# Transposing head rows in 32x32 blocks on VectorE, with the transfers to DRAM placing the blocks

## The chip, the cores and the metric

One core of a Trainium2 chip runs the whole kernel. The metric is device time in microseconds for one launch; lower is better. Engines are TensorE (PE; its weight loads are listed as PEld), VectorE (DVE), ScalarE (ACT), GpSimd (POOL) and SyncE (SP), which here issues nearly all transfers. Sixteen DMA engines move the data; their share in the profile is the mean over all of them.

## The reference

The reference computes one step of a decoder layer for 256 prompt tokens and 8 sequences of 8 sample tokens (320 tokens, D = 2048, float32). Two token mixers work on the same projection and are merged:

```python
proj = einsum('btd,de->bte', x, w_in)     # split into the heads' inputs and gates
h, C, n, m = _mlstm(q, k, v, ig, lf, C0, n0, m0)         # 4 heads, DK 256, DV 512
h = _unheads((h - mu) * rsqrt(var + eps)) * ml_norm_g
branch_a = h * sigmoid(ml_o)
o, S = _hgrn2(hq, log(f), 1 - f, i, S0)                  # 8 heads, DK 128, DV 256
o = _unheads(o * rsqrt(mean(o * o) + eps)) * hg_norm_g
branch_b = o * silu(hg_g)
merged = sigmoid(gate_a) * (branch_a @ w_branch_a) + sigmoid(gate_b) * (branch_b @ w_branch_b)
x1 = layernorm(alpha * x + merged @ w_out)
y = layernorm(alpha * x1 + relu(x1 @ w_up)**2 @ w_down)
```

The outputs are y and the last states of every head: for the prompt C (a sum over tokens of weighted key times value), n, m and S, and the same for the samples.

## The kernel before, in words

The weights stream through as 304 tiles of 2048 x 128 (`TILES`). A tile gives 128 output features for all 320 tokens: 16 steps along the contraction, and in each step three float32r products (high by high, low by high, high by low), 48 products of 320 columns. Half a tile, 512 KB, is one unit: SyncE loads it into one of three raw buffers (`wr`, `reload`), ScalarE writes its high part (`prep`, `wh`), VectorE its low part (`low_half`, `wl`), TensorE uses it (`run_main`, products recorded at line 340, `mm`). Later other buffers (`bb`) take the place of `wh` and `wl`.

The order of tiles: for each of the 4 mLSTM heads its values, keys and queries (`mv`, `mk`, `mq`) and two gate tiles; four more gate tiles; for each of the 8 HGRN heads two gate tiles and its inputs (`hf`, `hq`, `hi`); then the output gates (`o`), rest of the merge gates, `hg` with `wa`, `wb`, `wo`, and the feed-forward tiles `up` and `dn`.

Everything else is side work in chains (Python generators), which a planner (`Sched`) puts between the weight products on each engine, with estimated costs and due times. The order on each engine is thereby written out before launch; at run time an engine waits only on semaphores. SyncE's queue is in order too: a transfer whose data isn't ready holds up those behind it.

The tokens stand along the free axis of the projections, features along the partitions. A head's result has tokens along the partitions, and the branches need features there. So `turned`, called at the end of `m_sample` for the mLSTM rows and of `h_out` for the HGRN rows, turns blocks of 128 x 128 on TensorE (line 1280) into a PSUM bank. ScalarE evicts them, with the norm's weight of each feature (`vec`, columns `V_MLG` and `V_HGG`) as the scale, and SyncE stores them to DRAM (`hT`, `oT`). Samples of two heads share one block: an even head's sample rows wait in the third part of `hb` or `on` until the odd head's are added, and the odd head turns both. `fetch` reads the stored blocks back much later, when the output gates' tiles come (`ev_o`, `ev_hg`), where VectorE multiplies them with the gate.

The prompt's keys are turned too, for the last states: `m_KW` turns the weighted mLSTM keys (line 1072), splits them into high and low part, and `m_CP` stores them with the values (`kD`, `vD`); `h_sp` turns the HGRN keys (line 1671) and stores them in `sD`. The products of keys and values are made at the very end (`m_C`, which loads by GpSimd's queue, and `h_S`).

Line 334 is the helper `A` (every ScalarE activation), line 343 the helper `dma` (every SyncE transfer), line 502 the low part of a weight unit.

Of the kernel before, what the change touches and what calls it, by code (L numbers as in the profile page):

```python
# [20 lines left out]
TOK = 320  # L21
# [221 lines left out]
def rel(pool, item):  # L243
    return ("rel", pool, item)
# [51 lines left out]
class Program:  # L296
# [49 lines left out]
    def carve(self):  # L346
# [38 lines left out]
        self.vs = Pool([R(512)])  # L385
        self.khl = Pool([R(1024).rearrange("p (x s k) -> p x s k", x=2, s=2)])
        self.kst = Pool([R.three(2, 256)])
# [10 lines left out]
        self.on = Pool([self.on0])  # L398
        self.ho = Pool([B(320) for _ in range(2)])
        R2 = Part(self.ra, 5120)  # L400
# [13 lines left out]
    def carve_h(self):  # L414
        C = self.Part(self.pool.tile([128, F3], F32, name="f3h", tag="f3"))
        qz = C(ODD + 256)
        self.hqz = Pool([qz])
        pp = C(512)
        self.pp = Pool([pp])
        self.ktk = Pool([C.three(2, 128)])  # L420
# [236 lines left out]
    def start(self):  # L657
# [52 lines left out]
        self.gb_ev = [Ev() for _ in range(KT)]  # L710
        self.hT = [self.dr.tile([128, TOK], F32, name=f"hT{j}") for j in range(KT)]
        self.oT = [self.dr.tile([128, TOK], F32, name=f"oT{j}") for j in range(KT)]
        self.hT_ev = [Ev() for _ in range(KT)]
# [56 lines left out]
    def lb(self):  # L770
# [284 lines left out]
    def m_KW(self, h):  # L1055
# [12 lines left out]
        khl = yield acq(self.khl)  # L1068
        b = yield acq(self.sbank)
        for i in range(2):  # L1070
            for c in range(2):
                yield ("pe", PE_T, lambda: nc.tensor.transpose(b[:, 256 * i + 128 * c:256 * i + 128 * c + 128], kw[:, c, 128 * i:128 * i + 128], self.ident))  # L1072
# [104 lines left out]
    def m_C(self, h):  # L1177
        k = yield acq(self.kx)
        kt = yield ("pool", 1000, lambda: self.nc.gpsimd.dma_start(k, self.kD[h]))
        w = yield acq(self.vx)  # L1180
# [28 lines left out]
    def m_sample(self, h):  # L1209
# [54 lines left out]
        yield rel(self.sm, dn)  # L1264
        yield from self.turned(4, odd, hb, 4 * h, V_MLG, self.tst, self.hT, self.hT_ev)
        yield rel(self.hb, hb)
# [7 lines left out]

    def turned(self, n, odd, rows, j0, vec, pool, to, ev):

        for j in range(n):
            b = yield acq(self.sbank)
            for i in range(2 + odd):
                yield ("pe", PE_T, lambda: self.nc.tensor.transpose(b[:, 128 * i:128 * i + 128], rows[:, i, 128 * j:128 * j + 128], self.ident))  # L1280
            jj = j0 + j
            o = yield acq(pool)
            g = lambda i: self.vec[:, vec + i:vec + i + 1]
            yield ("act", act(NP_, True, 1), lambda: self.A(o[:, 0:NP_], b[:, 0:NP_], scale=g(jj)))
            if odd:
                yield ("act", act(64, True, 1), lambda: self.A(by_row(o, NP_, False), by_row(b, NP_ + ODD, True), scale=g(jj)))
                e = yield acq(pool)
                yield ("act", act(64, True, 1), lambda: self.A(by_row(e, 0, False), by_row(b, NP_, True), scale=g(jj - n)))
            yield rel(self.sbank, b)
            k = TOK if odd else NP_  # L1290
            yield ("sp", 620, lambda: self.dma(to[jj][:, 0:k], o[:, 0:k]))
            if odd:
                yield ("sp", 620, lambda: self.dma(to[jj - n][:, NP_:TOK], e[:, 0:64]))
                yield post(ev[jj])
                yield post(ev[jj - n])
            yield wait(self.later(2500))
            yield rel(pool, o)
            if odd:
                yield rel(pool, e)

# [359 lines left out]
    def h_sp(self, h):  # L1660
# [7 lines left out]
        yield ("dve", dve(256), lambda: v.tensor_tensor(ks, qk[:, 0, 0:256], ks, ALU.mult))  # L1668
        b = yield acq(self.sbank)
        for i in range(2):  # L1670
            yield ("pe", PE_T, lambda: nc.tensor.transpose(b[:, 128 * i:128 * i + 128], ks[:, 128 * i:128 * i + 128], self.ident))  # L1671
        kt = yield acq(self.ktk)
        yield ("act", act(256, True), lambda: self.A(kt, b[:, 0:256].rearrange("p (a k) -> p a k", a=2)))
        yield rel(self.sbank, b)
# [44 lines left out]
    def h_out(self, h):  # L1719
# [31 lines left out]
        yield rel(self.at, at)  # L1751
        yield from self.turned(2, h % 2, on, 2 * h, V_HGG, self.ho, self.oT, self.oT_ev)
        yield rel(self.on, on)
# [23 lines left out]
    def fetch(self, kind, j):  # L1777

        src, ev = dict(o=(self.hT, self.hT_ev), wa=(self.gaD, self.m_ev), hg=(self.oT, self.oT_ev), wb=(self.gbD, self.gb_ev))[kind]
        e = self.got[kind, j] = Ev()  # L1780
        yield wait(ev[j])
        x = self.met[kind, j] = yield acq(self.ld)
        e.t = (yield ("sp", 620, lambda: self.dma(x, src[j]))) + 3000.0

# [4 lines left out]
    def ev_o(self, j, c, b):  # L1789
# [35 lines left out]
    def ev_hg(self, j, c, b):  # L1825
# [273 lines left out]
    def run(self, pool):  # L2099
# [9 lines left out]
        self.s_ev, self.s_bank = [Ev() for _ in range(HH)], {}  # L2109
        self.sD = [self.dr.tile([128, 768], F32, name=f"sD{j}") for j in range(HH)]  # L2110
        self.kD = [self.dr.tile([128, 2, 2, 256], F32, name=f"kD{j}") for j in range(MH)]
        rows = lambda name, n, k: [self.dr.tile([32 * NB, k], F32, name=f"{name}{j}") for j in range(n)]
# [57 lines left out]
def take_out(r):  # L2170
# [4 lines left out]
        c(y[:NP_].reshape(1, NP_, D)), c(y[NP_:].reshape(NB, NT, D)),  # L2175
        c(r["Cp"].transpose(0, 2, 1, 3).reshape(1, 1, MH, DK, DV)),
        c(n[:, 0:8].reshape(128, MH, 2).transpose(1, 2, 0).reshape(1, 1, MH, DK)),
# [24 lines left out]
```

## Time and profile before

| what | value |
|---|---|
| median of 3 runs | 2295.9 us (2295.43 to 2297.25) |
| profiled execution, its own time | 2295.59 us |
| its span in the trace | 2293.8 us |
| TensorE busy | 2285.9 us, 15706 products |
| VectorE, ScalarE busy | 1403.3 us, 1028.2 us |
| granted TensorE clock | 0.999 |
| DMA packets, data moved | 158303, 434.98 MB |

A row of a group of instructions names line, engine, operation, output and inputs, shape and count, then the busy time of the group and the mean of one in ns, then the idle time of the engine before them and what ended it. In a tile's view a row shows the count, and minimum, median and maximum of the durations in ns. Matmuls are pipelined: durations of neighbours overlap, and the distance between starts is what one adds to the stream.

### The profile page before, as it was taken

What the parts mean: (1) busy time and instruction counts of PE and PEld (TensorE: products, weight loads), DVE (VectorE), ACT (ScalarE), POOL (GpSimd) and SP (SyncE); (2) the same over time, 40 slices, a digit from 0 to 9 for tenths busy, and PEclk for the clock granted to TensorE, in tenths of its full rate; (3) what the DMA queues carried; (4) which work ended last, traced back from release to release, by engine and by line L of the source; (5) the groups of instructions that cost most, each with busy time, mean ns of one, the idle gap of its engine ahead of it and who ended that gap; (6) DMA issues with size and microseconds to landing.
All of it is one profiled execution on the core that took longest, in us unless ns stands there. A gap on an engine that the chain in (4) does not pass through costs nothing.

```text
span 2293.8 us, 39115 instructions
## 1 busy us (share of the span) xinstructions
PE 2285.9 (100%) x15706; PEld 2248.9 (98%) x15706; DVE 1403.3 (61%) x2437; ACT 1028.2 (45%) x1606; POOL 11.3 (0%) x42
## 2 busy tenths in 40 slices
PE   9999999999999999999999999999999999999998
PEld 9999999999999999999999999999999999999998
DVE  7666657788878876555555769544444444444555
ACT  5344445555555555444433547433443343234434
POOL 0000000000000000000000000000000000000000
PEclk9999999999999999999999999999999999999999
DMA  7887876666666565555555654444444444444555
GB/s 239 314 273 263 290 253 206 200 214 204 202 208 223 186 195 175 174 176 172 170 174 185 215 159 143 153 152 151 147 151 153 147 149 154 148 148 153 192 188 184
DMA packets 158303, 434.98 MB, mean 190 GB/s; under 512 B 19868, under 2 KB 50724, under 8 KB 157096
## 3 DMA queue, kind: packets, MB, share of 16 engines
q1 hardware_dynamic: 156968, 426.18, 56.2%
q0 software_dynamic: 1152, 6.29, 0.8%
q8 instruction: 123, 2.02, 0.4%
q14 instruction: 60, 0.49, 0.1%
HBM read 376.25 MB, written 56.15 MB: 189 GB/s over the span
## 4 chain that ended last, share of the span: by engine, by line
PE 98%; DMA 1%; ACT 1%; DVE 0%; issue 0%; SPq 0%; ACTq 0%
PE bank L340 97%; DMA wr<-wt 1%; PE bank L1280 0%; ACT f3m L334 0%; DVE bb L502 0%; PE bank L1551 0%; PE bank L982 0%; ACT oC L334 0%; ACT bb L334 0%; PE bank L1018 0%; PE bank L1671 0%; PE bank L1099 0%; PE bank L1072 0%; ACT wh L334 0%; DVE wl L502 0%
## 5 line engine op out<-in xcount | busy, mean ns | idle before, releaser
L340 PE MATMUL bank<-xh,wh 128*128 128x320 f32 x2408 | 770.7, 321 | 0.2 <-ACT wh L334 0.2
L340 PE MATMUL bank<-xh,wl 128*128 128x320 f32 x2408 | 743.5, 310 | 0.0
L340 PE MATMUL bank<-xl,wh 128*128 128x320 f32 x2408 | 740.4, 309 | 0.0
L334 ACT ACTIVATE wh<-wr 128x1024 fp32r<-128x1024 f32 (+1 forms) x431 | 452.3, 1049 | 594.2 <-PE bank L340 579.9
L502 DVE TENSOR_TENSOR wl<-wr,wh 128x1024 fp32r<-128x1024 f32 x423 | 517.7, 1224 | 328.2 <-ACT wh L334 323.0
L340 PEld LDWEIGHTS bank<-xh,wh 128*128 128x128 f32 x2408 | 452.5, 188 | 7.7 <-issue 3.9
L340 PEld LDWEIGHTS bank<-xl,wh 128*128 128x128 f32 x2408 | 453.1, 188 | 2.6
L340 PEld LDWEIGHTS bank<-xh,wl 128*128 128x128 f32 x2408 | 452.9, 188 | 0.0
L334 ACT ACTIVATE bb<-wr 128x1024 fp32r<-128x1024 f32 x179 | 189.8, 1061 | 358.2 <-PE bank L340 343.0
L502 DVE TENSOR_TENSOR bb<-wr,bb 128x1024 fp32r<-128x1024 f32 x179 | 219.1, 1225 | 165.4 <-ACT bb L334 165.4
L340 PE MATMUL bank<-xh,bb 128*128 128x320 f32 (+1 forms) x1280 | 284.1, 309 | 0.0
L340 PE MATMUL bank<-ra,bb 128*128 128x320 f32 x1264 | 283.3, 308 | 0.0
L340 PE MATMUL bank<-rxb,bb 128*128 128x320 f32 x1112 | 255.0, 309 | 0.0
L340 PE MATMUL bank<-ra,wh 128*128 128x320 f32 x892 | 248.8, 308 | 0.0
L340 PEld LDWEIGHTS bank<-xh,bb 128*128 128x128 f32 x1280 | 214.7, 188 | 0.0
L340 PEld LDWEIGHTS bank<-ra,bb 128*128 128x128 f32 x1264 | 210.6, 188 | 0.2
L340 PE MATMUL bank<-xl,bb 128*128 128x320 f32 (+1 forms) x640 | 197.5, 309 | 0.0
L340 PEld LDWEIGHTS bank<-rxb,bb 128*128 128x128 f32 x1112 | 188.4, 188 | 0.2
L340 PE MATMUL bank<-rxb,wl 128*128 128x320 f32 x596 | 183.7, 308 | 0.0
L340 PE MATMUL bank<-rxb,wh 128*128 128x320 f32 x596 | 183.7, 308 | 0.0
L340 PEld LDWEIGHTS bank<-ra,wh 128*128 128x128 f32 x892 | 161.4, 188 | 0.0
L340 PEld LDWEIGHTS bank<-xl,bb 128*128 128x128 f32 x640 | 120.2, 188 | 0.0
(328 smaller groups left out, 2187.0 us busy)
## 6 DMA issues: line engine op xcount, KB each, us to landing
wr<-wt SPq DMA_DIRECT2D x602, 512.0 KB
rx<-C SPq DMA_DIRECT2D x34, 256.0 KB
Cs<-rx SPq DMA_DIRECT2D x34, 256.0 KB
f<-C SPq DMA_DIRECT2D x30, 256.0 KB
Cs<-f SPq DMA_DIRECT2D x30, 256.0 KB
f<-xT SPq DMA_DIRECT2D x26, 160.0 KB
vD<-ra SPq DMA_DIRECT2D x4, 1024.0 KB
f<-S SPq DMA_DIRECT2D x8, 512.0 KB
```

Source lines behind the costliest of these rows:

```text
L334: return self.nc.scalar.activation(out, in_, func, **kw)
L340: self.nc.tensor.matmul(*a, **kw)
L502: self.V().tensor_tensor(lo, raw, hi.bitcast(F32), ALU.subtract)
```

## The change

Prompt rows in `turned`, the mLSTM keys in `m_KW` and the HGRN keys in `h_sp` are no longer turned by TensorE. VectorE transposes within 32 x 32 blocks, SBUF to SBUF, and the store puts each block in its place in DRAM: one store for each group of 32 partitions, with runs of 32 elements (128 B), or 64 (256 B) for the mLSTM keys. Only the sample rows of a pair of heads still go through TensorE and ScalarE (in the odd head). The norms' weights are no longer a scale of the eviction; they are a factor in `ev_o` (there negated, in place of the constant -1) and `ev_hg`. `hT` and `oT` become one tensor for each head, `kD` holds the keys by token, `skD` is new and takes the HGRN keys out of `sD`. The mLSTM keys' channels stand in another order in `kD`, and the host puts the rows of C back in order.

```diff
@@ carve
-        self.tst = Pool([B(320) for _ in range(2)])
+        self.tst = Pool([B(512)])
+        self.tail = Pool([B(64) for _ in range(2)])
...
@@ lb
+        g = self.vec[:, V_MLG:V_MLG + 16]
+        yield ("dve", 80, lambda: nc.vector.tensor_scalar(g, g, -1.0, None, ALU.mult))
...
@@ m_KW
-        b = yield acq(self.sbank)
-        for i in range(2):
-            for c in range(2):
-                yield ("pe", PE_T, lambda: nc.tensor.transpose(b[:, 256 * i + 128 * c:256 * i + 128 * c + 128], kw[:, c, 128 * i:128 * i + 128], self.ident))
-        bv = b.rearrange("p (a k) -> p a k", a=2)
-        yield ("act", act(512, True), lambda: self.A(kh, bv))
-        yield ("dve", dve(512, True), lambda: v.tensor_tensor(kl, bv, kh.bitcast(F32), ALU.subtract))
-        yield rel(self.sbank, b)
+        by = lambda x, c: x.rearrange("p (b c e) -> p c b e", c=2, e=32)[:, c]
+        st = yield acq(self.stg)
+        for c in range(2):
+            x = kw[:, 0, 0:256] if c else st
+            yield ("dve", dve(256), lambda: v.transpose(x, kw[:, c, 0:256]))
+            x = x.rearrange("p (b e) -> p b e", e=32)
+            yield ("act", act(256), lambda: self.A(by(kh, c), x))
+            yield ("dve", dve(256), lambda: v.tensor_tensor(by(kl, c), x, by(kh, c).bitcast(F32), ALU.subtract))
+        yield rel(self.stg, st)
...
@@ m_CP
-        yield ("sp", 620, lambda: self.dma(self.kD[h], m["khl"].bitcast(F32)))
+        for x in range(2):
+            for a in range(4):
+                yield ("sp", 620, lambda: self.dma(
+                    self.kD[h][x].rearrange("(b r) k -> r b k", r=32)[:, :, 64 * a:64 * a + 64],
+                    m["khl"][32 * a:32 * a + 32, x, :].bitcast(F32).rearrange("r (b k) -> r b k", k=64)))
...
@@ m_C
-        kt = yield ("pool", 1000, lambda: self.nc.gpsimd.dma_start(k, self.kD[h]))
+        kt = yield ("pool", 1000, lambda: self.nc.gpsimd.dma_start(k, self.kD[h].rearrange("x (s p) k -> p x s k", s=2)))
...
@@ turned, new body
+        v = self.nc.vector
+        o = yield acq(pool)
+        for i in range(2):
+            x = o if i == 0 else rows[:, 0, :]
+            yield ("dve", dve(128 * n), lambda: v.transpose(x, rows[:, i, :]))
+            for a in range(4):
+                at = 128 * i + 32 * a
+                yield ("sp", 620, lambda: self.dma(
+                    to[-1].rearrange("(b r) t -> r b t", r=32)[:, :, at:at + 32], x[32 * a:32 * a + 32].rearrange("r (b t) -> r b t", t=32)))
+        t = self.later(2500)
+        for j in range(n if odd else 0):
             b = yield acq(self.sbank)
+            yield ("pe", PE_T, lambda: self.nc.tensor.transpose(b[:, 0:128], rows[:, 2, 128 * j:128 * j + 128], self.ident))
+            for k in range(2):
+                e = yield acq(tail)
+                yield ("act", act(64, True), lambda: self.A(by_row(e, 0, False), by_row(b, ODD * (1 - k), True)))
+                if k:
+                    yield rel(self.sbank, b)
+                yield ("sp", 620, lambda: self.dma(to[-1 - k][128 * j:128 * j + 128, NP_:TOK], e))
+                self.s.spawn(self.back(tail, e), 0)
...
@@ h_sp
-        for i in range(2):
-            yield ("pe", PE_T, lambda: nc.tensor.transpose(b[:, 128 * i:128 * i + 128], ks[:, 128 * i:128 * i + 128], self.ident))
-        yield ("act", act(256, True), lambda: self.A(kt, b[:, 0:256].rearrange("p (a k) -> p a k", a=2)))
-        yield ("sp", 620, lambda: self.dma(self.sD[h][:, 0:256], kt))
-        yield ("sp", 620, lambda: self.dma(self.sD[h][:, 256:768], m["iv"][:, 0:512]))
+        yield ("dve", dve(256), lambda: v.transpose(kt, ks))
+        for a in range(4):
+            p = slice(32 * a, 32 * a + 32)
+            yield ("sp", 620, lambda: self.dma(self.skD[h].rearrange("(b r) k -> r b k", r=32)[:, :, p], kt[p].rearrange("r (b k) -> r b k", k=32)))
+        yield ("sp", 620, lambda: self.dma(self.sD[h], m["iv"][:, 0:512]))
...
@@ h_S
-        t = yield ("sp", 620, lambda: self.dma(x, self.sD[h]))
+        yield ("sp", 620, lambda: self.dma(x[:, 0:256].rearrange("p (i k) -> p i k", i=2), self.skD[h].rearrange("(i p) k -> p i k", i=2)))
+        t = yield ("sp", 620, lambda: self.dma(x[:, 256:768], self.sD[h]))
...
@@ ev_o
-        yield ("dve", dve(TOK), lambda: v.scalar_tensor_tensor(g, g, -1.0, x, ALU.mult, ALU.mult))
+        yield ("dve", dve(TOK), lambda: v.scalar_tensor_tensor(g, g, self.vec[:, V_MLG + j:V_MLG + j + 1], x, ALU.mult, ALU.mult))
...
@@ ev_hg
-        yield ("dve", dve(TOK), lambda: v.tensor_tensor(g, g, x, ALU.mult))
+        yield ("dve", dve(TOK, ptr=1), lambda: v.scalar_tensor_tensor(g, g, self.vec[:, V_HGG + j:V_HGG + j + 1], x, ALU.mult, ALU.mult))
```

More of the change, by code (lines that the diff above doesn't have):

```diff
@@ L398, in carve @@
         self.on = Pool([self.on0])
-        self.ho = Pool([B(320) for _ in range(2)])
+        self.ho = Pool([B(256) for _ in range(2)])
+        self.tail2 = Pool([B(64) for _ in range(2)])
         R2 = Part(self.ra, 5120)
@@ L419, in carve_h @@
         self.pp = Pool([pp])
-        self.ktk = Pool([C.three(2, 128)])
+        self.ktk = Pool([C(256)])
         R = self.Part(self.pool.tile([128, 2320], F32R, name="f2r", tag="f2a"))
@@ L710, in start @@
         self.gb_ev = [Ev() for _ in range(KT)]
-        self.hT = [self.dr.tile([128, TOK], F32, name=f"hT{j}") for j in range(KT)]
-        self.oT = [self.dr.tile([128, TOK], F32, name=f"oT{j}") for j in range(KT)]
+        self.hT = [self.dr.tile([512, TOK], F32, name=f"hT{j}") for j in range(MH)]
+        self.oT = [self.dr.tile([256, TOK], F32, name=f"oT{j}") for j in range(HH)]
         self.hT_ev = [Ev() for _ in range(KT)]
@@ L1264, in m_sample @@
         yield rel(self.sm, dn)
-        yield from self.turned(4, odd, hb, 4 * h, V_MLG, self.tst, self.hT, self.hT_ev)
+        yield from self.turned(4, odd, hb, self.tst, self.tail, self.hT[h - odd:h + 1], self.hT_ev[4 * h - 4:4 * h + 4])
         yield rel(self.hb, hb)
@@ L1273, in m_sample @@
             yield ("sp", 620, lambda: self.dma(self.d["n_out"][:, 8:72], self.nso_flat))
-    def turned(self, n, odd, rows, j0, vec, pool, to, ev):
-        for j in range(n):
-            b = yield acq(self.sbank)
[L1279 to L1299, printed above, removed]
@@ new lines, in turned @@
+    def turned(self, n, odd, rows, pool, tail, to, ev):
+        v = self.nc.vector
[9 more added lines that the diff above has]
+        for j in range(n if odd else 0):
+            b = yield acq(self.sbank)
+            yield ("pe", PE_T, lambda: self.nc.tensor.transpose(b[:, 0:128], rows[:, 2, 128 * j:128 * j + 128], self.ident))
[6 more added lines that the diff above has]
+                self.s.spawn(self.back(tail, e), 0)
+        if odd:
+            for x in ev:
+                yield post(x)
+        yield wait(t)
+        yield rel(pool, o)
@@ L1301, in m_done, with back @@
+    def back(self, pool, x):
+        yield wait(self.later(2500))
+        yield rel(pool, x)
     def m_done(self, h, name, evs, pool):
@@ L1751, in h_out @@
         yield rel(self.at, at)
-        yield from self.turned(2, h % 2, on, 2 * h, V_HGG, self.ho, self.oT, self.oT_ev)
+        yield from self.turned(2, h % 2, on, self.ho, self.tail2, self.oT[h - h % 2:h + 1], self.oT_ev[2 * h - 2:2 * h + 2])
         yield rel(self.on, on)
@@ L1782, in fetch @@
         x = self.met[kind, j] = yield acq(self.ld)
[L1783 removed]
+        n = len(src)
+        y = src[j * n // KT]
+        o = 128 * (j % (KT // n))
+        e.t = (yield ("sp", 620, lambda: self.dma(x, y[o:o + 128, :]))) + 3000.0
     def fetched(self, kind, j):
@@ L2109, in run @@
         self.s_ev, self.s_bank = [Ev() for _ in range(HH)], {}
-        self.sD = [self.dr.tile([128, 768], F32, name=f"sD{j}") for j in range(HH)]
-        self.kD = [self.dr.tile([128, 2, 2, 256], F32, name=f"kD{j}") for j in range(MH)]
+        self.sD = [self.dr.tile([128, 512], F32, name=f"sD{j}") for j in range(HH)]
+        self.skD = [self.dr.tile([256, 128], F32, name=f"skD{j}") for j in range(HH)]
+        self.kD = [self.dr.tile([2, 256, 256], F32, name=f"kD{j}") for j in range(MH)]
         rows = lambda name, n, k: [self.dr.tile([32 * NB, k], F32, name=f"{name}{j}") for j in range(n)]
@@ L2175, in take_out @@
         c(y[:NP_].reshape(1, NP_, D)), c(y[NP_:].reshape(NB, NT, D)),
-        c(r["Cp"].transpose(0, 2, 1, 3).reshape(1, 1, MH, DK, DV)),
+        c(r["Cp"].reshape(MH, 2, 2, 32, 2, DV).transpose(0, 2, 4, 1, 3, 5).reshape(1, 1, MH, DK, DV)),
         c(n[:, 0:8].reshape(128, MH, 2).transpose(1, 2, 0).reshape(1, 1, MH, DK)),
```

4 lines of the change are left out of this document (1 added, 3 removed).

## The prediction

> **What bounds the kernel now.** I read the page first, then the busy time by stretches, then the single products in the timeline, and last the transfers.
>
> ```profile
> span 2293.8 us, 39115 instructions
> PE 2285.9 (100%) x15706; PEld 2248.9 (98%) x15706; DVE 1403.3 (61%) x2437; ACT 1028.2 (45%) x1606; POOL 11.3 (0%) x42
> PE 98%; DMA 1%; ACT 1%; DVE 0%; issue 0%; SPq 0%; ACTq 0%
> ```
>
> TensorE carries 98% of the chain that ended last. A busy share of 100% could still hide waiting, because products overlap, so the pace has to be looked at.
>
> ```profile
> 57.00:115.00 58.00, 58.00 (x398) 52.83 (x398) 36.86 (x73) 23.30 (x39) 0.00 (x0) 1.00 0.89 315
> 115.00:229.00 114.00, 114.00 (x789) 108.49 (x787) 73.18 (x148) 51.90 (x92) 0.00 (x0) 1.00 0.80 268
> 459.00:573.00 114.00, 114.00 (x812) 111.69 (x811) 93.24 (x247) 60.82 (x127) 0.88 (x3) 1.00 0.64 209
> 1400.00:1700.00 300.00, 300.00 (x2048) 300.00 (x2047) 156.01 (x206) 124.09 (x170) 0.00 (x0) 1.00 0.47 151
> ```
>
> The columns are the stretch, its length, then busy time and count of PE, PEld, DVE, ACT and POOL, the granted clock, the DMA share and GB/s. From 1400 to 1700 us there are only weight products: 300 us by 2048 is 0.1465 us for one. The stretches from 57 to 573 us are where the changed work lies (mLSTM heads, then HGRN heads). There TensorE has no idle stretch either, VectorE is busy up to 82% (93.24 of 114) and the 16 DMA rings up to 0.89. So every instruction taken off TensorE there is time, as long as the weights still come in time. The weights are what the rest must not disturb.
>
> **The transposes that go.** These are the groups of transposes in question:
>
> ```profile
> L1280 PE MATMUL bank<-cst,f 128*128 128x128 f32 x80 | 21.7, 271 | 0.0
> L1671 PE MATMUL bank<-cst,f 128*128 128x128 f32 x12 | 3.3, 272 | 0.0
> L1072 PE MATMUL bank<-cst,f2a 128*128 128x128 f32 x16 | 4.3, 272 | 0.0
> L1671 PE MATMUL bank<-cst,f3h 128*128 128x128 f32 x4 | 1.1, 272 | 0.0
> ```
>
> That is 80 in `turned`, 16 for the mLSTM keys, 12 and 4 for the HGRN keys: 112. The changed `turned` keeps a transpose for the sample rows of a pair of heads: 4 blocks by 2 odd mLSTM heads and 2 blocks by 4 odd HGRN heads, 16. So 96 go. A duration of 271 ns isn't the price of one, since the next product starts long before its end; the starts tell it:
>
> ```profile
> 126.04 0.31 PE L340 MATMUL bank<-xh,wl 128*128 128x320 f32 x1
> 126.19 0.27 PE L982 MATMUL bank<-cst,f 128*128 128x128 f32 x1
> ...
> 128.41 0.31 PE L340 MATMUL bank<-xh,wh 128*128 128x320 f32 x1
> ...
> 132.72 0.27 PE L982 MATMUL bank<-cst,f 128*128 128x128 f32 x1
> 132.82 0.27 PE L1280 MATMUL bank<-cst,f 128*128 128x128 f32 x1
> ```
>
> From 126.04 to 128.41 the stream holds 13 weight products and 4 single transposes. 2.37 us less 13 by 0.1465 leaves 0.466, so 0.116 for a transpose between products; two in a row start 0.10 apart. I take 0.11, with 0.10 and 0.12 as bounds: 96 by 0.11 is 10.6 us (9.6 to 11.5). All of it is on the path. The Trainium skill (TensorE: Matmul & The Clock Gate, Part 4: PE-mode transpose) puts a transpose at about 275 ns in a kernel. The duration column here agrees (271), and by it the sum would be 26 us; the starts contradict it as a price in a stream.
>
> ScalarE loses the evictions behind them and TensorE's banks are freed sooner; ScalarE isn't on the path, so I count neither.
>
> **VectorE.** No 32x32 block transpose is in this trace. The nearest rows:
>
> ```profile
> L985 DVE TENSOR_TENSOR ra<-bank,ra 128x512 fp32r<-128x512 f32 x8 | 5.5, 689 | 5.2 <-ACT ra L334 5.1
> L1459 DVE TENSOR_TENSOR f<-f 128x256 f32<-128x256 f32 x12 | 5.0, 419 | 0.2 <-PE bank L340 0.2
> L822 DVE RECIPROCAL f<-f 4x320 f32<-4x320 f32 x1 | 2.1, 2134 | 0.0
> ```
>
> Added are 8 transposes 512 wide (two for each mLSTM head's rows) and 32 that are 256 wide (two for its keys, two for an HGRN head's rows, one for its keys). At elementwise speed, 0.69 and 0.42, that is 19 us in all, 1.3 us for an HGRN head, whose six tiles of weights alone take 42 us (288 products by 0.1465). The dearest row per element, the reciprocal with 6.7 ns, would make it 3.4 and 1.7 us each, 82 us in all. I take the elementwise price, the commoner by far. Nothing could make VectorE gain from it. What hides it is the lead of the weights, worked out next; even one transpose of 3.4 us in front of a weight's low half is shorter than that lead. The norm weights' part is free: an elementwise operation gets a pointer where it had a constant, or another input, and no instruction is added but one on 16 columns.
>
> **The lead of the weights.** A half tile of weights (512 KB) is loaded, split by ScalarE and VectorE, and used. The shortest lead in the mLSTM stage stands where the rings are full:
>
> ```profile
> 92.42 0.33 SPq L343 DMA_DIRECT2D wr<-wt  x1
> 99.89 1.06 ACT L334 ACTIVATE wh<-wr 128x1024 fp32r<-128x1024 f32 x1 [2.69 <-PE bank L340]
> 100.98 1.23 DVE L502 TENSOR_TENSOR wl<-wr,wh 128x1024 fp32r<-128x1024 f32 x1 [2.52 <-ACT wh L334]
> 107.61 0.30 PE L340 MATMUL bank<-xh,wh 128*128 128x320 f32 x1
> ...
> q1 hardware_dynamic: 1931, 4.37, 101.6%
> ```
>
> The last row is the DMA view from 90 to 102 us: the rings had no room at all. Even so the split ended at 102.21, and the first product that needs it (counted off at 24 products for a half tile) started at 107.61. So a load may come 5.4 us later than now before TensorE waits. This is the cover of everything that follows.
>
> **The transfers.** For each mLSTM head, 4 stores of rows become 8, each in 512 runs of 128 B, and one store of keys becomes 8, each in 256 runs of 256 B. For each HGRN head, 2 stores become 8 and one becomes 4, each in 256 runs of 128 B. Each odd head has as many stores of sample rows again as before. They wait on SyncE's queue for VectorE's transposes, and the loads of the weights stand behind them. That queue has time: its longest waits are for VectorE's split.
>
> ```profile
> SPq L343 <- DVE wl L502: 882.4, 320, 7.7
> ...
> L343 SPq DMA_DIRECT2D ksD<-ra x32: 570/577/595, 428.8 to 768.7; - x32
> L343 SPq DMA_DIRECT2D ra<-vsDm x4: 371/378/575, 66.6 to 316.0; - x4
> L343 SPq DMA_DIRECT2D hT<-f x24: 320/380/1044, 128.7 to 413.3; - x24
> ```
>
> A plain store takes the queue from 0.32 us. `ksD`, which goes out in blocks of 8 rows, takes 0.577, and `vsDm`'s load in two runs for a partition 0.378. A scattered store isn't in the trace. From below it costs 0.32 us. From above I take the step from one run to two, 0.05 us at least, for each further run: 16 runs make 0.32 and 15 by 0.05, 1.08 us. I take 0.58, the blocked store's. Eight in a row hold a load up for 4.6 us, less than 5.4.
>
> For the rings the nearest row is a moment in which almost only 256 B runs of sample rows move, into the same kind of tensor (717.70 to 717.98 us):
>
> ```profile
> DMA packets 144, 0.03 MB, mean 117 GB/s; under 512 B 144, under 2 KB 144, under 8 KB 144
> q1 hardware_dynamic: 144, 0.03, 53.5%
> ```
>
> 53.5% of 16 engines for 0.28 us is 2.40 us over 144 packets: 16.6 ns. A 128 B run should cost no more, and half of that at least. Eight stores of 512 runs then take 8 by 512 by 16.6 ns by 1/16, 4.2 us of all rings, beside the issues and not on top. All 49152 runs together are 51 us of the rings; in the stages from 115 us on, with 0.64 to 0.80 busy, there is room. The Trainium skill (DMA: Bandwidth & Descriptors, Specifications) wants at least 512 B, since the DMA engine reads, modifies and writes below that. The 256 B row shows no such jump; what twice its price would do is a rival below.
>
> Who reads the scattered data does so late: `hT` is read from 768 us on, written until 413; `kD` at the end, by GpSimd's queue:
>
> ```profile
> L343 SPq DMA_DIRECT2D f<-hT x16: 322/425/607, 768.2 to 879.7; - x16
> 2258.27 0.53 POOL L1179 DMA_DIRECT2D wh<-kD  x1 [27.48 <-PE bank L340]
> ```
>
> Its four loads become 512 runs of 1 KB instead of 128 of 4 KB; the last two heads' products come over 10 us after that issue, so even 5 us more would not show. One more load for each HGRN state hides likewise.
>
> **The sum.** Minus 10.6 us. The profiled execution took 2295.6 us, its span of 2293.8 and 1.8 around it; the median of the runs is 2295.9, 0.3 above it. So 2295.9 less 10.6 is 2285.3 us. About 0.2% (4.6 us) is what can be told from no change.
>
> **Rivals.**
> - SyncE's queue gives it back. At 1.08 us a scattered store of 16 runs, eight in a row hold a load up for 8.6 us, 3.2 beyond the lead, for 4 heads 13 us; the stores of 8 runs (0.67 us) stay within it. 2298 us, no change that can be told. It eats the whole gain from 1.0 us a store. For it speaks that blocked stores cost 0.25 us more than plain ones; against it that VectorE's second transpose and waiting weight loads come between the eight. Chance 0.11.
> - Each short run costs twice the row, 33 ns. Eight stores of 512 runs then take 8.4 us, 3.0 beyond the lead for each of 4 heads, 12 us: less 10.6, that is 1.4 us slower than now, 2297.3, no change. The rule on 512 B named above reads this way if its extra pass costs as much as the write; the 256 B row doesn't show one. Chance 0.04.
> - The rings choke on short runs, slower than before. At 50 ns for a 128 or 256 B run, three times the row, eight stores take 12.8 us for an mLSTM head's rows (7.4 beyond the lead, 4 times) and 6.4 us for the keys and an HGRN head's rows (1.0 beyond, 12 times): 41.6 less 10.6, 2327 us. Slower by over 0.2% from 36 ns. For it speak the full rings from 90 to 102 us and that runs this short were never written in number; against it the 16.6 ns. Chance 0.16.
> - A transpose takes its whole duration from the stream: 96 by 0.271 is 26 us, 2269.9. The starts 0.10 apart speak against it. Chance 0.02.
>
> **How the numbers follow.** The forecast has 0.67. Its own range is 2282 (every transpose at 0.12, and a few of the present small delays gone with them) to 2291, where the lead is overrun by a microsecond or so at a few heads. With the rivals: faster 0.69, same 0.15, slower 0.16. The range starts at 2282 and reaches to 2304, which takes in the queue's case, the doubled one and of the rings' case the part up to 39 ns; some 0.13 is left out above and 0.03 below.
>
> **What would show it.** TensorE's instructions fall by 96 to 15610, with weight products still at 0.1465 us in the mLSTM and HGRN stages, and the span is near 2283. VectorE shows 40 transposes at 0.4 and 0.7 us. The scattered stores take the queue under 0.7 us. DMA packets rise to some 210 thousand and the DMA share of 115 to 573 us by less than 0.1. I am wrong if TensorE waits for splits (its idle time named after ScalarE or VectorE) or if ScalarE's splits wait for `wt` in these stages: then by the queue if its stores take 1 us, by the rings if loads land late while the queue is idle.

## The result, and the profile after

| | before | after |
|---|---|---|
| median | 2295.9 us | 2285.5 us (5 runs, 2285.44 to 2287.74) |
| ratio after to before | | 0.9956, 95% interval 0.9941 to 0.9971 |
| profiled execution, its span | 2295.59 us, 2293.8 us | 2287.74 us, 2286.0 us |

The changed kernel is 10.4 us faster (the interval gives 6.7 to 13.5); 2285.3 was forecast. The execution that was profiled is the longest of the five, 2.2 us above the median; a second profile of the same kernel (`e0_after` below) has a span of 2283.3 us. The page of the first, its head, its queue and its chain of work that ended last:

```profile
span 2286.0 us, 39135 instructions
PE 2276.7 (100%) x15610; PEld 2239.0 (98%) x15610; DVE 1417.0 (62%) x2482; ACT 1009.6 (44%) x1570; POOL 12.3 (1%) x42
DMA packets 209694, 434.97 MB, mean 190 GB/s; under 512 B 73308, under 2 KB 103140, under 8 KB 208488
q1 hardware_dynamic: 206824, 426.19, 57.4%
PE 96%; DMA 2%; ACT 1%; DVE 0%; SPq 0%; issue 0%; ACTq 0%
```

TensorE has 96 instructions fewer, VectorE 14 us more, ScalarE 19 us less, and there are 51 thousand more packets for the same bytes. TensorE still carries the chain. The stretches in which the changed work lies, with the columns as before (stretch, length, PE, PEld, DVE, ACT, POOL, clock, DMA share, GB/s):

```profile
57.00:115.00 58.00, 57.41 (x388) 51.77 (x386) 39.24 (x83) 24.53 (x42) 0.00 (x0) 1.00 0.97 335
115.00:229.00 114.00, 114.00 (x785) 108.23 (x784) 78.76 (x161) 49.98 (x86) 0.00 (x0) 1.00 0.83 264
459.00:573.00 114.00, 114.00 (x809) 111.84 (x808) 94.80 (x257) 56.77 (x116) 0.88 (x3) 1.00 0.68 213
1400.00:1700.00 300.00, 300.00 (x2049) 300.00 (x2048) 152.77 (x195) 120.26 (x161) 0.00 (x0) 1.00 0.46 151
```

In the rows from 115 us on TensorE has no idle stretch, and the rings are at 0.83 and 0.68 where they were at 0.80 and 0.64. The first row lacks 0.59 us of TensorE; that is one wait, taken up below. The new operations, first the groups and then the tiles' rows of SyncE's queue (count, then minimum, median and maximum ns of one issue):

```profile
L1301 PE MATMUL bank<-cst,f 128*128 128x128 f32 x16 | 4.3, 271 | 0.0
L1293 DVE STREAM_TRANSPOSE f<-f 128x256 f32<-128x256 f32 x16 | 7.0, 439 | 0.0
L1293 DVE STREAM_TRANSPOSE f<-f 128x512 f32<-128x512 f32 x8 | 5.6, 702 | 0.0
L1688 DVE STREAM_TRANSPOSE f3h<-f 128x256 f32<-128x256 f32 x6 | 2.6, 439 | 0.0
...
L343 SPq DMA_DIRECT2D hT<-f x48: 319/424/1529, 127.2 to 398.6; - x48
L343 SPq DMA_DIRECT2D oT<-f x80: 302/442/1200, 463.8 to 818.8; - x80
L343 SPq DMA_DIRECT2D kD<-ra x32: 302/442/1498, 65.7 to 319.5; - x32
L343 SPq DMA_DIRECT2D skD<-f3h x32: 326/442/657, 432.7 to 779.5; - x32
```

**Where the time went.** Weight products are the same in both kernels and come in the same order, so the start of the k-th one can be compared. These are timeline rows of the 145th and the 4801st weight product, with nearly all of the changed work between them; first before, then after:

```profile
30.52 0.31 PE L340 MATMUL bank<-xh,wh 128*128 128x320 f32 x1
...
830.46 0.30 PE L340 MATMUL bank<-xh,wh 128*128 128x320 f32 x1
```

```profile
32.68 0.42 PE L340 MATMUL bank<-xh,wh 128*128 128x320 f32 x1 [0.46 <-ACT f L334]
...
823.01 0.30 PE L340 MATMUL bank<-xh,wh 128*128 128x320 f32 x1
```

Before, the stretch between them took 799.94 us, after 790.33: 9.61 less, and the 0.59 us wait is in that. The stream starts 2.16 us later in the second. Of the changed instructions only VectorE's new one on 16 columns lies ahead of that point (0.17 us at 25.74 us); `e9_norms`, which has it too, starts only 0.27 us later than before. The same stretch was read from every profile below ("the stretch", always against 799.94):

| kernel | transposes fewer | the stretch | median against before on the same chip |
|---|---|---|---|
| before, second profile | 0 | +0.1 | |
| e9_norms | 0 | -0.3 | +0.8 |
| e1_put_back | 0 | +0.3 | +1.1 |
| e2_keys | 32 | -3.6 | -2.4 |
| e3_rows | 64 | -6.4 | -5.8 |
| e4_plain | 96 | -6.2 | -4.3 |
| after, first profile | 96 | -9.6 | -10.4 |
| after, second profile | 96 | -11.3 | -9.8 |
| e5_dve5 | 96 | -10.0 | -8.3 |
| e6_issues | 96 | -10.4 | -9.4 |
| e7_twice | 96 | -7.0 | -8.0 |
| e10_long_runs | 96 | -11.3 | -10.3 |
| e8_tails | 112 | -12.7 | -11.8 |

The stretch belongs to one execution and holds that execution's waits; the medians also hold the start. The two profiles of the changed kernel differ by 1.7 us: the first loses 0.65 us at the wait named above and 1.0 us at 93 us, where products that read `f` come late.

### The profile page after: what moved, and what is told of

It reads as the page before. It is cut to its first block, busy times and chain, and to the rows that moved or that the text cites. A ratio compares the mean times of both kernels' runs of the same rounds, so it can differ in the third digit from the quotient of the medians.

```text
span 2286.0 us, 39135 instructions
## 1 busy us (share of the span) xinstructions
PE 2276.7 (100%) x15610; PEld 2239.0 (98%) x15610; DVE 1417.0 (62%) x2482; ACT 1009.6 (44%) x1570; POOL 12.3 (1%) x42
## 3 DMA queue, kind: packets, MB, share of 16 engines
q1 hardware_dynamic: 206824, 426.19, 57.4%
## 4 chain that ended last, share of the span: by engine, by line
PE 96%; DMA 2%; ACT 1%; DVE 0%; SPq 0%; issue 0%; ACTq 0%
PE bank L340 96%; DMA wr<-wt 1%; ACT f3m L334 0%; DMA f<-xT 0%; DMA ra<-vsDm 0%; DMA f<-C 0%; SPq L343 0%; DVE wl L504 0%; DMA rx<-wt 0%; PE bank L1569 0%; PE bank L986 0%; ACT oC L334 0%; ACT wh L334 0%; PE bank L1301 0%; PE bank L1022 0%
```

## Experiments

The theory: the gain is TensorE's 96 instructions alone, at what one adds to the stream; all that was added is hidden. Rivals: something else gives it (ScalarE's lost evictions, the norms' weights), or a part of the gain is eaten by SyncE's queue, by VectorE or by short runs on the rings, and a better form would bring more.

**The transposes put back.** The changed kernel with 96 transposes into a bank that nobody reads; ScalarE's evictions stay away.

```diff
@@ turned
+        for j in range(n):
+            b = yield acq(self.sbank)
+            for i in range(2):
+                yield ("pe", PE_T, lambda: self.nc.tensor.transpose(b[:, 128 * i:128 * i + 128], rows[:, i, 128 * j:128 * j + 128], self.ident))
+            yield rel(self.sbank, b)
...
@@ m_KW: the same with four transposes of kw; h_sp: the same with two of ks
```

> The changed kernel with 96 TensorE transposes put back at the places where they were (8 for each mLSTM head's rows, 4 for its keys, 4 for an HGRN head's rows, 2 for its keys), into a bank that nobody reads; VectorE's transposes and the scattered stores stay. Theory (the gain is TensorE's stream time, 0.11 us a transpose): all of it goes, 2285.5 + 10.4 = 2296 us, within 1 us. Rival (the gain comes from ScalarE's evictions and from banks held shorter): under 2289 us, since those stay away.

Measured: 2297.1 us (2295.87 to 2300.65) against 2295.98, ratio 1.0008 (0.9999 to 1.0017). The whole gain is gone, with ScalarE as in the changed kernel:

```profile
PE 2286.8 (100%) x15706; PEld 2249.4 (98%) x15706; DVE 1419.9 (62%) x2482; ACT 1011.4 (44%) x1570; POOL 12.6 (1%) x42
```

So ScalarE's 19 us are worth nothing, and the gain sits in TensorE's instruction count. At 2297.1 us it lies 0.1 us above what was expected, and 1.1 us above the kernel before on the same chip.

**Keys alone, rows alone.** `e2_keys` has the changed keys (`m_KW`, `m_CP`, `h_sp`) and `turned` as before, `e3_rows` the reverse.

```diff
@@ e2_keys: turned, as before
-            yield ("dve", dve(128 * n), lambda: v.transpose(x, rows[:, i, :]))
+                yield ("pe", PE_T, lambda: self.nc.tensor.transpose(b[:, 128 * i:128 * i + 128], rows[:, i, 128 * j:128 * j + 128], self.ident))
...
@@ e3_rows: m_KW and h_sp, as before
-            yield ("dve", dve(256), lambda: v.transpose(x, kw[:, c, 0:256]))
+                yield ("pe", PE_T, lambda: nc.tensor.transpose(b[:, 256 * i + 128 * c:256 * i + 128 * c + 128], kw[:, c, 128 * i:128 * i + 128], self.ident))
```

> The kernel before with only the keys changed (mLSTM and HGRN keys by VectorE and scattered stores), rows as before: 32 transposes fewer. Theory: 32 by 0.11 is 3.5 us, 2292.4 us, less the 0.6 us for which TensorE waited on the values' load behind the keys' stores: 2292 to 2293.5. Rival (the keys' stores, which fall into the fullest stage, cost more than they bring): 2296 us or more, and the rows would bring all of the gain.

> The changed kernel with the keys as before (TensorE, plain stores); only the rows and the norms' weights are changed: 64 transposes fewer. Theory: 64 by 0.11 is 7.0 us, 2288.9 us, within 0.7; with the keys alone it adds up to the whole change. Rival (keys cost more than they bring): 2285 us or less.

Measured: keys 2293.57 us (2292.75 to 2295.01), ratio 0.9989 (0.9980 to 0.9998); rows 2290.19 us (2288.65 to 2292.14), ratio 0.9974 (0.9964 to 0.9984); before 2295.98. Both bring something, the rows more, as their counts of 32 and 64 say. But both come out above what was expected (2293.5 and 2289.6 us at most), and 2.4 and 5.8 make 8.2 us of the 10.4. In the profile of rows alone stands a wait that no other profile has:

```profile
PE bank L1103 <- DVE f L1040: 0.8, 1, 0.8
```

Each kernel is planned anew, so TensorE's side work lands elsewhere, and one of its products can come ahead of its data. The 0.8 us accounts for part of the missing 2.2; the rest was not taken apart. By the stretch the halves bring 3.6 and 6.4 us, 10.8 with that wait added, which lies between the 9.6 and 11.3 us of the whole.

**Fewer issues, long runs.** One plain store in place of each four scattered ones (two groups of four for the mLSTM keys): 124 stores and 39 thousand packets fewer than in the changed kernel. The data is then misplaced inside `hT`, `oT`, `kD` and `skD`, so y and the states' products are computed on blocks in the wrong place.

```diff
@@ turned (m_CP and h_sp alike)
-            for a in range(4):
-                at = 128 * i + 32 * a
-                yield ("sp", 620, lambda: self.dma(
-                    to[-1].rearrange("(b r) t -> r b t", r=32)[:, :, at:at + 32], x[32 * a:32 * a + 32].rearrange("r (b t) -> r b t", t=32)))
+            yield ("sp", 620, lambda: self.dma(
+                to[-1].rearrange("(j p) t -> p j t", p=128)[:, :, 128 * i:128 * i + 128], x[:, 0:128 * n].rearrange("p (j t) -> p j t", t=128)))
```

> The changed kernel with each group of four scattered stores replaced by one plain store of the same bytes (for rows and keys, runs of 512 B or 1 KB; the blocks then stand in the wrong places, so the output's values are not the reference's). It takes away some 110 issues and 45 thousand packets. Theory (the scattered stores are hidden but for the wait behind the first keys): 2285 us, 0 to 1.0 us below the changed kernel. Rival (the scattered stores eat some of a gain that was larger): 2 us or more below, 2283 or less.

Measured: 2291.69 us (2289.02 to 2294.1), ratio 0.9980 (0.9971 to 0.9989). With less work in the queue and on the rings it is 6 us slower than the changed kernel. Neither theory has that. Its longest waits of TensorE, and two slices behind the first of them (columns as above, the clock third from the right):

```profile
PE bank L340 <- DMA ra<-vsDm: 2.1, 1, 2.1
PE bank L340 <- DVE f L1475: 1.4, 1, 1.4
...
81.00:82.00 1.00, 1.00 (x7) 0.96 (x4) 0.97 (x2) 0.00 (x0) 0.00 (x0) 0.50 0.12 49
83.00:84.00 1.00, 1.00 (x5) 1.00 (x5) 0.55 (x1) 0.00 (x0) 0.00 (x0) 0.50 0.87 303
```

The planner counts 0.62 us for each issue. With fewer of them it plans other times, and two side products come 2.1 and 1.4 us ahead of what they read. Right behind the first wait the granted clock is 0.50 from 81 to 84 us (0.87 and 0.92 in the slices beside), which loses another 1.7 us; behind the second it stays at 1.00. That makes 5.2 us, about what the stretch lacks against the changed kernel's second profile (11.3 less 6.2). All this confounds the experiment: it changed the order, too. It was therefore made again with the same number of issues, below (`e10_long_runs`).

**The changed kernel again.** No edit; is the wait of 0.59 us part of the change?

> The changed kernel once more, beside the next three and with a second profile. In its first profile the stream's first 144 products ended 2.2 us later than in the kernel before, ahead of all changed work, and TensorE waited 0.59 us for the values' load (vsDm) behind the first keys' stores. Theory: the late start is chance from one execution to the next, so this one has a median of 2285 to 2286.5 us and another delay at the start; the wait at 78 us stays, 0.3 to 1 us. Rival: the change itself delays the start, again by 2 us or more.

Measured: 2285.72 us (2285.11 to 2286.92) against 2295.51, ratio 0.9957 (0.9943 to 0.9970). The waits of TensorE in the first profile and then in this one:

```profile
PE bank L340 <- POOL ones L666: 1.0, 1, 1.0
PE bank L340 <- DMA f<-xT: 0.6, 1, 0.6
PE bank L340 <- DMA ra<-vsDm: 0.6, 1, 0.6
PE bank L340 <- ACT f L334: 0.5, 1, 0.5
```

```profile
PE bank L340 <- POOL ones L666: 1.0, 1, 1.0
PE bank L340 <- ACT f L334: 0.5, 1, 0.5
```

The wait for `vsDm` is gone: it was expected to stay, and that was wrong. In the first profile scattered stores of keys stand ahead of that load in SyncE's order, which looked like the cause:

```profile
70.02 0.33 SPq L343 DMA_DIRECT2D kD<-ra  x1
71.33 0.39 SPq L343 DMA_DIRECT2D ra<-vsDm  x1
...
78.10 0.50 PE L340 MATMUL bank<-ra 32*128 32x512 f32 x4 [0.59 <-DMA ra<-vsDm]
```

But the second profile has the same order and no wait, and the kernel before has the wait in its own second profile:

**The kernel before again.** No edit.

> The kernel before, for a second profile. All profiles of changed kernels ended the first 144 products 0.8 to 3.1 us later than the one profile of before, and none has its wait of 0.65 us at 1285 us. Theory (both are chance from one execution to the next): here the first 144 products end 0.5 to 2 us later than in the first profile, or the wait at 1285 is gone. Rival: both stand as in the first profile, so that the changes cause the late start.

```profile
PE bank L340 <- POOL ones L664: 1.0, 1, 1.0
PE bank L340 <- DMA f<-xT: 0.8, 1, 0.8
PE bank L340 <- DMA ra<-vsDm: 0.5, 1, 0.5
```

One execution, 2296.43 us, span 2294.7. Its stream starts 1.64 us later than in the first profile of the same kernel, and the wait at 1285 us is gone, both as expected. So lateness of up to 2 us at the start and single waits of half a microsecond in the first 80 us differ between executions of one kernel, and no profile shows that any of it belongs to the change: the changed kernel's second profile starts 0.41 us ahead of this one.

**VectorE five times.** Each block transpose is made five times.

```diff
@@ turned (m_KW and h_sp alike)
-            yield ("dve", dve(128 * n), lambda: v.transpose(x, rows[:, i, :]))
+            for _ in range(5):
+                yield ("dve", dve(128 * n), lambda: v.transpose(x, rows[:, i, :]))
```

> The changed kernel with each of VectorE's block transposes done five times over: 160 transposes more, by the profile 4 times 19.7 us, 79 us on VectorE. Theory (VectorE has room and the weights have a lead of about 5 us): 2285 to 2289 us. Rival (VectorE, 82% busy in the HGRN stage, is next in line): 4 times 1.3 us for each HGRN head, of which half or more shows: 2305 us or more.

Measured: 2287.18 us (2286.54 to 2288.99), ratio 0.9962 (0.9950 to 0.9975).

```profile
L1295 DVE STREAM_TRANSPOSE f<-f 128x512 f32<-128x512 f32 x40 | 28.2, 706 | 0.6
PE 2276.1 (100%) x15610; PEld 2237.5 (98%) x15610; DVE 1474.5 (65%) x2642; ACT 1014.4 (44%) x1570; POOL 12.3 (1%) x42
```

Four times the added transposes once more, 79 us by their durations and 58 us of VectorE's busy time (1474.5 against 1417.0; those in a row overlap), cost 1.5 us beside the changed kernel's 2285.72 on the same chip; shared evenly, one set costs 0.4 us. In this and the next two experiments TensorE's order was planned anew, too, so a part of each difference may be the order's.

**Twice the issues.** Each scattered store goes out in two halves, 160 issues more (the expectation counted 128) with the same runs.

```diff
@@ turned (m_CP and h_sp alike)
-                yield ("sp", 620, lambda: self.dma(
-                    to[-1].rearrange("(b r) t -> r b t", r=32)[:, :, at:at + 32], x[32 * a:32 * a + 32].rearrange("r (b t) -> r b t", t=32)))
+                for q in (slice(0, 2 * n), slice(2 * n, 4 * n)):
+                    yield ("sp", 620, lambda: self.dma(
+                        to[-1].rearrange("(b r) t -> r b t", r=32)[:, q, at:at + 32], x[32 * a:32 * a + 32, 0:128 * n].rearrange("r (b t) -> r b t", t=32)[:, q, :]))
```

> The changed kernel with each scattered store cut in two of half as many runs: the same packets, 128 issues more on SyncE's queue, some 0.4 us each. Theory (the queue has room, the lead covers bursts): only what stands behind the first keys' stores gets later: 2286 to 2290 us. Rival (SyncE's queue is the next bound): 128 by 0.4 is 51 us, and half of it shows: 2310 us or more.

Measured: 2286.13 us (2285.25 to 2286.45), ratio 0.9956 (0.9944 to 0.9969).

```profile
L343 SPq DMA_DIRECT2D oT<-f x144: 302/430/1452, 462.2 to 841.7; - x144
```

Sixteen of these are stores of sample rows, as before. Half as many runs in a store take the queue 0.430 us at the median where the whole store took 0.442 (`kD` and `skD`, which hold scattered stores alone, show the same), so the issue's price hardly goes by the number of runs. The 160 more cost 0.4 us in all, less than the runs spread.

**Twice the short runs.** Each scattered store is made a second time into a tensor that nobody reads: 160 issues (again counted as 128 in the expectation) and 49 thousand short packets more.

```diff
@@ turned (m_CP and h_sp alike)
-                yield ("sp", 620, lambda: self.dma(
-                    to[-1].rearrange("(b r) t -> r b t", r=32)[:, :, at:at + 32], x[32 * a:32 * a + 32].rearrange("r (b t) -> r b t", t=32)))
+                for w in (to[-1], self.xD[n]):
+                    yield ("sp", 620, lambda: self.dma(
+                        w.rearrange("(b r) t -> r b t", r=32)[:, :, at:at + 32], x[32 * a:32 * a + 32].rearrange("r (b t) -> r b t", t=32)))
```

> The changed kernel with each scattered store made twice, the second into scratch tensors: 128 issues and 49 thousand short packets more. Theory (both queue and rings are covered; the rings' price is at most 16.6 ns a packet): as with the issues alone and at most 2 us more, 2286 to 2292 us. Rival (short runs are dear for the rings, 36 ns or more each): eight stores twice take 18 us of the rings, four times, so 2320 us or more.

Measured: 2287.55 us (2286.82 to 2290.57), ratio 0.9967 (0.9954 to 0.9979). The profiled execution is the one of 2290.57:

```profile
57.00:115.00 58.00, 57.95 (x393) 52.56 (x391) 39.39 (x85) 24.59 (x42) 0.00 (x0) 1.00 1.01 345
115.00:229.00 114.00, 112.98 (x769) 106.03 (x768) 77.83 (x158) 49.46 (x85) 0.00 (x0) 1.00 0.89 274
...
PE bank L340 <- DMA f<-C: 1.0, 1, 1.0
ACT wh L334 <- DMA wr<-wt: 17.7, 13, 3.7
```

Now the rings are full from 57 to 115 us (1.01), TensorE once waits 1.0 us for a late load of a state (at 173 us), and ScalarE waits up to 3.7 us for weights, still without TensorE waiting for a split. Even so it costs 1.8 us by the medians. The rings have room for what the change adds, though not much more in the mLSTM stage.

**The norms' weights alone.** The kernel before, with the weights moved from the evictions into `ev_o` and `ev_hg`.

```diff
@@ turned (the samples' evictions alike), ev_hg; ev_o and lb as in the change
-            yield ("act", act(NP_, True, 1), lambda: self.A(o[:, 0:NP_], b[:, 0:NP_], scale=g(jj)))
+            yield ("act", act(NP_, True), lambda: self.A(o[:, 0:NP_], b[:, 0:NP_]))
...
-        yield ("dve", dve(TOK), lambda: v.tensor_tensor(g, g, x, ALU.mult))
+        yield ("dve", dve(TOK, ptr=1), lambda: v.scalar_tensor_tensor(g, g, self.vec[:, V_HGG + j:V_HGG + j + 1], x, ALU.mult, ALU.mult))
```

> The kernel before with only the norms' weights moved from the evictions into the gates' products; TensorE turns all as before. Theory: no change, 2295.5 within 1 us, as no engine gets an instruction but one on 16 columns. Rival (ScalarE's evictions with a scale held something up, 0.09 us each): 2 us or more faster.

Measured: 2296.53 us (2294.65 to 2298.39) against 2295.7, ratio 1.0003 (0.9994 to 1.0011): no change. This part is free and gives nothing.

**Long runs in the same order.** As many issues as in the changed kernel, each from the same 32 partitions, but in runs of 512 B or more, with data misplaced as in `e4_plain`; TensorE's order is that of the changed kernel.

```diff
@@ turned (m_CP and h_sp alike)
-                    to[-1].rearrange("(b r) t -> r b t", r=32)[:, :, at:at + 32], x[32 * a:32 * a + 32].rearrange("r (b t) -> r b t", t=32)))
+                    to[-1].rearrange("(j p) t -> p j t", p=128)[32 * a:32 * a + 32, :, 128 * i:128 * i + 128], x[32 * a:32 * a + 32, 0:128 * n].rearrange("r (j t) -> r j t", t=128)))
```

> The changed kernel with every scattered store writing the same 32 partitions in long runs (512 B, 1 KB for the mLSTM keys) instead of 128 or 256 B: as many issues in the same order, TensorE's order the same instruction for instruction, only the runs are longer and the blocks stand in the wrong places, so the values are not the reference's. Theory (short runs are covered): 2285.6 us less 0 to 0.7. Rival (short runs cost the stream what the plain stores seemed to hide): 2 us or more below the changed kernel, 2283.6 or less.

Measured: 2285.4 us (2284.69 to 2287.06), ratio 0.9955 (0.9941 to 0.9968).

```profile
DMA packets 172830, 434.97 MB, mean 191 GB/s; under 512 B 24156, under 2 KB 66276, under 8 KB 171624
q1 hardware_dynamic: 169960, 426.19, 56.9%
```

Beside the changed kernel's 2285.5 and 2285.72 the scattering costs 0.1 to 0.3 us by the medians, less than the runs spread (2.4 us), so that no cost of it is shown. The stretch equals that of the changed kernel's second profile (both -11.3). This also settles `e4_plain`: with the order kept, the 6 us are gone.

**One step further.** If only TensorE's count matters, the 16 sample transposes should go, too. `e8_tails` turns the samples' rows on VectorE as well and stores them in runs of 8 elements, 32 B.

```diff
@@ turned
-        for j in range(n if odd else 0):
-            b = yield acq(self.sbank)
-            yield ("pe", PE_T, lambda: self.nc.tensor.transpose(b[:, 0:128], rows[:, 2, 128 * j:128 * j + 128], self.ident))
...
+        if odd:
+            y = rows[:, 1, :]
+            yield ("dve", dve(128 * n), lambda: v.transpose(y, rows[:, 2, :]))
             for k in range(2):
...
+                for a in range(4):
+                    for r in range(2):
+                        at, q = NP_ + 32 * r + 8 * a, ODD * (1 - k) + 8 * r
+                        yield ("sp", 620, lambda: self.dma(
+                            to[-1 - k].rearrange("(b r) t -> r b t", r=32)[:, :, at:at + 8],
+                            y[32 * a:32 * a + 32].rearrange("r (b t) -> r b t", t=32)[:, :, q:q + 8]))
```

> The changed kernel taken further: the sample rows too are transposed by VectorE and placed by stores in runs of 32 B (16 stores for a pair of heads instead of 8 or 4), so that the last 16 transposes of the rows leave TensorE. Theory: 16 by 0.11 is 1.7 us, 2283.9 us, if the stores stay covered (64 issues and 29 thousand short packets more). Rival (a new wait behind the stores takes it back): 2285.5 us or more.

Measured: 2283.86 us (2283.5 to 2286.38) against 2295.7, ratio 0.9948 (0.9936 to 0.9961). By its median this version beats both kernels, by 11.8 us and by 1.6 to 1.9. The changed kernel did not run on this chip, but `e10_long_runs` with the same order did: 1.5 us more. The runs of these overlap, so the step from the changed kernel is likely rather than shown.

```profile
PE 2273.7 (100%) x15594; PEld 2236.3 (98%) x15594; DVE 1418.8 (62%) x2488; ACT 1008.8 (44%) x1538; POOL 12.3 (1%) x42
DMA packets 239390, 434.97 MB, mean 191 GB/s; under 512 B 103004, under 2 KB 132836, under 8 KB 238184
```

## Why the prediction was right, point by point

- **The bound.** TensorE's stream sets the time, so an instruction off it is time: right, and shown both ways, by putting the transposes back (1.1 us above the kernel before on the same chip, so the whole gain is gone) and, less surely, by taking 16 more away (1.6 to 1.9 us by the medians).
- **The price of a transpose.** Forecast 0.11 us, 10.6 in all, from the starts and not from the duration of 0.271 us. Measured 10.4 and 9.8 us by the medians, 0.10 to 0.11 for one; the stretch gives 11.3 in the second profile, 0.118 for one, within the bounds of 0.10 to 0.12. The rival with the whole duration (26 us) is refuted: the duration column is a price only where nothing overlaps.
- **VectorE.** The elementwise rows were the right ones: 0.439 and 0.702 us against 0.42 and 0.69. That its time is hidden holds: five times as much cost 1.5 us.
- **The cover.** This step was misread. The prediction took 5.4 us as the shortest lead of the weights in the mLSTM stage, at the place where the rings were full. Counted off in the same way for every half tile, the kernel before has 3.1 us at the one used from 60.9 us. The changed kernel has 1.5 us in its first profile (used from 62.7 us) and 0.06 us in its second, where the low part was done at 122.74 us and the first product that needs it started at 122.80:

```profile
121.54 1.20 DVE L504 TENSOR_TENSOR wl<-wr,wh 128x1024 fp32r<-128x1024 f32 x1
122.80 0.30 PE L340 MATMUL bank<-xh,wh 128*128 128x320 f32 x1
```

  One of the prediction's signs of being wrong came, too: ScalarE's splits wait for `wt`. Over the whole run, before, then the changed kernel's two profiles:

```profile
ACT wh L334 <- DMA wr<-wt: 6.2, 5, 1.7
ACT wh L334 <- DMA wr<-wt: 12.7, 14, 2.0
ACT wh L334 <- DMA wr<-wt: 15.5, 15, 2.9
```

  From 57 to 229 us alone that is 1.3 us before, then 5.3 and 9.4. No wait of TensorE for a split follows in either profile, so the time doesn't show it; with 3.1 us of lead the 4.6 us that the prediction gave eight stores in a row would not have been covered. That the weights came in time is therefore in part luck. With long runs in the same order these waits are 2.3 us and the shortest lead is 1.4 us; whether the short runs delay the weights stays open, since the changed kernel's own two profiles differ as much at one half tile (1.95 and 0.06 us).
- **SyncE's queue.** The term was mis-sized on the dear side: a scattered store takes 0.42 to 0.44 us at the median, not 0.58 (single ones up to 1.53). The upper bound of 1.08 was far off, since its step of 0.05 us "for each further run" isn't there: half as many runs take 0.430 where all take 0.442. The rival by which the queue gives the gain back needed 1.0 us; with 160 issues more the kernel lost 0.4 us.
- **The rings.** The shares rose by 0.03 (115 to 229 us), 0.07 (229 to 344 us) and 0.04 (459 to 573 us), as forecast below 0.1; from 57 to 115 us they went from 0.89 to 0.97, which left no more than that. With long runs in the same order they are 0.81, 0.84, 0.64 and 0.96, so the length of the runs makes up 0.01 to 0.04 of it. No price of one run comes out of this: the queue's share is 57.4% in the changed kernel's first profile and 55.6% in its second, and with long runs 56.9%, between the two. The choking rival would need 36 ns a run; it is refuted by `e7_twice`, and the rival of the doubled price is not borne out.
- **The rest.** Norms' weights and ScalarE counted for nothing, shown by `e9_norms` and `e1_put_back`. GpSimd's loads of the keys take 0.75 to 0.88 us to issue where they took 0.53 to 0.66, and no wait of TensorE names them.
- **What the prediction did not have.** It took the order of everything else as fixed. It is planned anew with every edit, and waits of 0.8 to 2.1 us appear where a side product lands ahead of its data: 3.5 us in `e4_plain`, with 1.7 us more by the lowered clock behind one of them, and some of the 2.2 us by which the two halves fall short of the whole. The changed kernel happened to have none of that kind; that was luck the range covered, not a step. The span of "near 2283" is met by the second profile (2283.3), missed by the first (2286.0), which starts 0.9 us later and loses the 1.7 us named above, both by chance from one execution to the next.

## What to carry to other kernels

Where TensorE's stream is the bound, price an instruction by the distance between starts, and look for a transpose that another engine can do in blocks and a store can finish, if its reader comes late. Before trusting a difference of a few microseconds, compare the k-th instruction of the unchanged stream in both traces, and take a second profile of each kernel: it separates the change from chance. In a kernel whose order is planned, keep the order when one cost is to be tested, or the experiment measures the plan. And where a lead is to cover what is added, take the shortest over all the places it must cover; the fullest moment of the rings need not be the one.

## What the runs showed of the hardware

A store that splits 32 partitions into 8 or 16 runs each took SyncE's queue 0.42 to 0.44 us at the median, where the plain ones before took 0.33 to 0.43. 41 thousand runs of 128 B and 8 thousand of 256 B could not be told from runs of 512 B and more in the time (2285.5 and 2285.72 against 2285.4). Thirty thousand packets more, most of them of 32 B, went with a share of the queue of 58.2%, where two profiles of the changed kernel have 57.4 and 55.6%. A 32x32-block transpose of float32 on VectorE goes at elementwise speed, 0.439 us for 128x256 and 0.702 for 128x512. Right behind a wait of 2.1 us TensorE's granted clock was 0.50 for 3 us (`e4_plain`); behind waits of 1.0 us (`e7_twice`) and 1.4 us it stayed at 1.00.
